# The prompt's W_down as seven block products instead of eight, its combinations made elsewhere

## The chip, the cores and the metric

The kernel runs on one core of a Trainium2 chip. The metric is the time of one execution in device microseconds; a kernel's time is the median of several runs. One further execution was recorded by the hardware profiler. All profile rows of this document come from such recorded executions, and their times count from the start of the recorded span.

The core has five engines with queues of their own: TensorE (PE in the profile, with its weight loads as PEld), VectorE (DVE), ScalarE (ACT), GpSimd (POOL), and SyncE (SP), which here issues most of the DMA transfers and computes nothing. Each engine works through a queue of its own, and what orders one queue against another are semaphores.

## The reference, cut to what matters

One encoder layer runs over two requests, a sample of 512 tokens and a prompt of 1024, with shared weights. The part that this change touches is the MLP at the end of the layer:

```
a = relu(rmsnorm(x, g_mlp) @ w_up)          # (T, 1024) @ (1024, 4096)
y = rmsnorm(x + (a * a) @ w_down, g_final)  # (T, 4096) @ (4096, 1024)
```

Everything is float32. The kernel gets this precision by writing each operand as a sum of two rounded parts, `hi` and `lo`, and by making three matmuls of each product (hi x hi, hi x lo, lo x hi) into one float32 sum.

## The kernel before, in words

The sample runs first, then the prompt. In the order of time the stages that matter are: the sample's MLP (class `Mlp`), in which W_up and W_down alternate in groups of two hidden tiles; the prompt's attention and branches; and the prompt's output projection, W_up and W_down (class `Halves`).

**Splitting.** Both parts of a weight are made on the core. `weights` (L140 ff.) takes one of two buffers named `w_raw` (`wtile`, two buffers for each kind, shared by the whole kernel), loads 512 KB into it by a DMA on SP (L144), and calls `split_sb`: ScalarE writes the rounded copy `hi` (L150), and then GpSimd, or VectorE where `lo_engine` says so, writes `lo` = raw - `hi` (L151). The raw buffer is free when both have read it. `mm3` (L127) issues the three matmuls for each pair of operands.

**The sample's MLP.** `Mlp.run` issues the W_up products of two hidden tiles, and then `down` for the group of two before them. `down` loads the two W_down tiles through `weights`, multiplies, and adds each 128x512 bank of PSUM to an accumulator in SBUF on VectorE (L1080). In every group one tile of the prompt is read, normed and transposed as well.

**The prompt's W_up** (`Halves.up`, from L1346) already works by seven block products instead of eight: halves of the tokens times halves of the inner dimension, in Winograd's form of Strassen's scheme. GpSimd makes the combinations of the weight's quarters beside the products (`prepare`, L1259), ScalarE and GpSimd split them. The result of a group of two hidden tiles is in two tiles `r` and `r_`; after relu and square (L1386) each of them, 128 hidden values by 1024 tokens, is written to DRAM (L1387).

**The prompt's W_down** (`Halves.down`, from L1389) goes over the 32 hidden tiles in 16 groups of two. For each tile it loads the hidden values (128x1024, `lo` on VectorE) and the rows of W_down (128x1024, `lo` on GpSimd). The loads of a group are issued one group ahead, into four pairs of `hi` and `lo` for each kind; the very first go into tiles of the stage before (`take`). A group has 8 token tiles x 2 column halves = 16 banks of six matmuls each, and VectorE adds every bank to an accumulator in SBUF (L1418). The last group adds the final norm (`norm`, L172 to L182) and the output transfers on SP.

**What sets the order.** The program is written in one order, and a planner with estimated durations puts each engine's instructions into its queue: the earliest in the program that it believes to be ready goes next. So an instruction whose operands come late can be passed by a later one, but only at planning time. `pinned` and `behind` tie instructions to a place behind others; `high_priority` moves some ahead. How many buffers a tile's name has is given as `bufs`; a new tile of that name waits until an older one is free.

Of the kernel before, what the change touches and what calls it, by code (L numbers as in the profile page):

```python
# [17 lines left out]
F32 = mybir.dt.float32  # L18
# [8 lines left out]
D = 1024  # L27
# [41 lines left out]
class Layer:  # L69
    def __init__(self, tc, ctx, ins, outs):  # L70
        self.tc, self.nc, self.ins, self.outs = tc, tc.nc, ins, outs
        self.turn = ["mm", "s", "o"]
        self.fn_ready = []
        nc = self.nc
        self.const = ctx.enter_context(tc.tile_pool(name="const", bufs=1))
        self.dram = ctx.enter_context(tc.tile_pool(name="scratch", bufs=1, space=DRAM))
        self.ps = ctx.enter_context(tc.tile_pool(name="ps", bufs=1, space=PSUM))
        self.ident = self.const.tile([128, 128], F32, name="ident")
        make_identity(nc, self.ident)
        self.zero = self.const.tile([128, 8], F32, name="zero")  # L80
# [6 lines left out]
        self.meta_values = None  # L87
        self.lanes = (mybir.EngineType.SP, mybir.EngineType.Activation, mybir.EngineType.Pool, mybir.EngineType.DVE)


# [934 lines left out]
    class Mlp:  # L1025
# [12 lines left out]
        def up(self, f):  # L1038
# [8 lines left out]
            for c in range(T // step):  # L1047
# [7 lines left out]
                nc.vector.tensor_tensor(out=lo[:, cs], in0=r, in1=hi[:, cs].bitcast(F32), op=ALU.subtract)  # L1055
# [45 lines left out]
class Halves:  # L1101

    TH = 512
    NF = FF // 128
    G = 2

    def __init__(self, layer, name, T):
        self.layer, self.nc, self.name, self.T = layer, layer.nc, name, T  # L1110
        self.x = layer.ins[f"x_{name}"]
        self.nt = T // 128
        assert T == 2 * self.TH
        self.sums = [layer.dram.tile([128, D], F32, name=f"sum_{name}{t}") for t in range(self.nt)]
        self.hid = [layer.dram.tile([128, T], F32, name=f"hidden_{name}{f}") for f in range(self.NF)]

    def run(self, right, hp, mp, m, wo):
        layer = self.layer
# [227 lines left out]
    def up(self, mp):  # L1346

        layer, nc, TH = self.layer, self.nc, self.TH
        for g in range(self.NF // 2):
# [32 lines left out]
                pass  # L1382
            nc.scalar.activation(out=r[:, right], in_=r[:, right], func=AF.Relu)
            nc.scalar.activation(out=r_, in_=r_, func=AF.Relu)
            for i, x in enumerate((r, r_)):
                nc.vector.tensor_tensor(out=x, in0=x, in1=x, op=ALU.mult)  # L1386
                nc.sync.dma_start(self.hid[2 * g + i], x)  # L1387

    def down(self, p):  # L1389

        layer, nc, nt, G = self.layer, self.nc, self.nt, self.G
        w, h = {}, {}

        def load(f):
            for x, of, src, lo_engine in (("h", h, self.hid[f], nc.vector), ("w", w, layer.ins["w_down"][f * 128:(f + 1) * 128, :], None)):
                of[f] = layer.weights(src, self.take(2) if f < G else layer.pair(p, [128, D], x, 2 * G), lo_engine=lo_engine)

        for f in range(G):
            load(f)
# [3 lines left out]
        for g in range(self.NF // G):  # L1403
            fs = range(g * G, (g + 1) * G)
            last = fs[-1] == self.NF - 1
            if not last:
                for f in range((g + 1) * G, (g + 2) * G):
                    load(f)
            else:
                gain = layer.gain(p.tile([128, D], F32, name="gain"), "g_final")  # L1410
            for t in range(nt):
                ts = slice(t * 128, (t + 1) * 128)
                for half in range(2):
                    cs = slice(half * 512, (half + 1) * 512)
                    ps = layer.psum()
                    layer.mm3(ps, [(h[f][0][:, ts], h[f][1][:, ts], w[f][0][:, cs], w[f][1][:, cs]) for f in fs])
                    with layer.tc.high_priority(offset=60) if last and t == nt - 1 else nullcontext():
                        nc.vector.tensor_tensor(out=acc[t][:, cs], in0=acc[t][:, cs], in1=ps, op=ALU.add)  # L1418
                if last:
                    o = p.tile([128, D], F32, name="out", bufs=2)  # L1420
                    with layer.tc.high_priority(offset=60) if t == nt - 1 else nullcontext():
                        layer.norm(acc[t], gain, o, junk=p.tile([128, D], BF16, name="junk"))
                    nc.sync.dma_start(layer.outs[self.name][t * 128:(t + 1) * 128, :], o)


def build(tc, ins, outs, order=(("sample", 512), ("prompt", 1024))):
# [84 lines left out]
```

## Time and profile before

| | us |
|---|---|
| median of 3 runs | 2089.66 |
| lowest, highest | 2088.76, 2090.30 |
| profiled execution: its time | 2087.42 |
| profiled execution: its span | 2085.6 |

| engine | busy us | share of the span |
|---|---|---|
| PE | 1999.6 | 96% |
| DVE | 1104.8 | 53% |
| ACT | 704.2 | 34% |
| POOL | 803.6 | 39% |

The recorded span begins and ends a little inside the execution, so the execution's time is 1.8 us above it. Busy shares are averages over stages with different limits. A busy TensorE in this table also says little of how fast its matmuls follow each other: records of matmuls overlap (in the prompt's W_down each is 0.39 us long, and they start 0.23 us apart). The distance between starts is what counts. In rows of a timeline the columns are start and duration in us, the engine, the line of the kernel, the operation with the tile it writes and those it reads, their shapes, and in brackets how long the engine stood idle before it and what ended that. "x4" is a count of like instructions merged into one row, and the duration is then that of all of them. SPq is the queue of SP; the duration there is that of issuing, not that of the transfer.

### The profile page before, as it was taken

The numbers are of one execution on the slowest core, as the hardware profiler recorded it, in microseconds if no ns is written. First come the engines' busy times: TensorE is split into PE (matmuls) and PEld (weight loads), VectorE is DVE, ScalarE is ACT, GpSimd is POOL, SyncE is SP. The second block draws the span as 40 slices with busy tenths as digits, with TensorE's granted clock in tenths as the row PEclk, the third lists the DMA queues.
The fourth block names the chain that finished last, engine by engine and source line by source line (L and its number), as shares of the span: only waits on it lengthen the run. The fifth ranks groups of instructions, "written<-read, shape, count | busy, mean of one in ns | idle before, by whom it ended". The sixth has DMA issues, their size and how long they took to land.

```text
span 2085.6 us, 26699 instructions
## 1 busy us (share of the span) xinstructions
PE 1999.6 (96%) x9803; PEld 1661.5 (80%) x9803; DVE 1104.8 (53%) x2031; ACT 704.2 (34%) x1270; POOL 803.6 (39%) x670
## 2 busy tenths in 40 slices
PE   6789979999999999999999999999999999999997
PEld 4777867878888878888888897877888888888886
DVE  6572435656565454466661328374323336656567
ACT  3464413333332323456642223133333332112112
POOL 2344525243444421333342226027777662222220
PEclk9999999999999999999999999999999999999998
DMA  6555872233433345555463453323323325323322
GB/s 207 163 132 186 224 221 91 82 114 110 123 99 92 94 149 183 130 136 138 122 219 99 128 157 112 118 91 101 107 95 121 107 88 209 108 84 102 100 90 92
DMA packets 244899, 267.25 MB, mean 128 GB/s; under 512 B 41048, under 2 KB 195416, under 8 KB 244216
## 3 DMA queue, kind: packets, MB, share of 16 engines
q1 hardware_dynamic: 231040, 244.67, 37.5%
q0 software_dynamic: 13728, 20.88, 4.2%
q8 instruction: 77, 1.26, 0.3%
q14 instruction: 54, 0.44, 0.1%
HBM read 210.24 MB, written 57.82 MB: 129 GB/s over the span
## 4 chain that ended last, share of the span: by engine, by line
PE 84%; DVE 8%; DMA 3%; ACT 2%; issue 1%; POOL 1%; SPq 1%; DVEq 0%; ACTq 0%; POOLq 0%
PE ps_mm L127 23%; PE ps_o L127 23%; PE ps_s L127 19%; PE ps_t L127 4%; PE ps_mm L491 3%; PE ps_mm L492 3%; PE ps_mm L493 3%; PE ps_o L621 2%; PE ps_t L604 1%; DVE hn L870 1%; DVE gate L875 1%; DMA gain<-in_w_fnB 1%; DMA w_raw<-in_w_out 1%; PE ps_s L591 1%; PE ps_s L592 1%
## 5 line engine op out<-in xcount | busy, mean ns | idle before, releaser
L151 POOL TENSOR_TENSOR w_lo<-w_raw,w_hi 128x1024 fp32r<-128x1024 f32 x141 | 347.0, 2466 | 670.8 <-ACT w_hi L150 620.8
L150 ACT CAST w_hi<-w_raw 128x1024 fp32r<-128x1024 f32 x142 | 147.2, 1047 | 281.2 <-DMA w_raw<-in_w_up 78.2
L1053 DVE TENSOR_TENSOR relu<-relu 128x512 f32<-128x512 f32 (+1 forms) x34 | 78.6, 2312 | 120.5 <-ACT relu L1052 120.5
L491 PE MATMUL ps_mm<-hT,w_hi 128*128 128x512 f32 (+3 forms) x312 | 122.3, 392 | 0.0
L492 PE MATMUL ps_mm<-hT,w_hi 128*128 128x512 f32 (+3 forms) x312 | 112.6, 361 | 0.0
L493 PE MATMUL ps_mm<-hT,w_lo 128*128 128x512 f32 (+3 forms) x312 | 112.5, 361 | 0.0
L150 ACT CAST h_hi<-w_raw 128x1024 fp32r<-128x1024 f32 x30 | 31.5, 1050 | 230.5 <-DMA w_raw<-hidden_prompt 77.3
L598 ACT ACTIVATE sc<-sc,ast 128x288 f32<-128x288 f32 (+4 forms) x96 | 53.8, 561 | 78.5 <-DVE ast L596 78.2
L1418 DVE TENSOR_TENSOR acc<-acc,ps_s 128x512 f32<-128x512 f32 x85 | 58.3, 686 | 39.8 <-PE ps_s L127 39.8
L1418 DVE TENSOR_TENSOR acc<-acc,ps_o 128x512 f32<-128x512 f32 x86 | 59.0, 686 | 38.5 <-PE ps_o L127 38.5
L1418 DVE TENSOR_TENSOR acc<-acc,ps_mm 128x512 f32<-128x512 f32 x85 | 58.3, 686 | 39.3 <-PE ps_mm L127 39.2
L1259 POOL TENSOR_TENSOR x<-w_hi,x 128x512 fp32r<-128x512 f32 (+1 forms) x42 | 63.8, 1519 | 39.5 <-ACT x L1262 39.5
L621 PEld LDWEIGHTS ps_o<-pt,vb 104*64 104x64 f32 (+6 forms) x576 | 63.5, 167 | 11.9 <-ACT pt L131 3.8
L621 PE MATMUL ps_o<-pt,vb 104*64 104x128 f32 (+6 forms) x576 | 66.2, 250 | 5.7 <-ACT pt L131 2.9
L604 PE MATMUL ps_t<-ident,sc 128*104 128x128 f32 (+3 forms) x288 | 50.5, 287 | 17.7 <-DVE pt L132 14.8
L561 POOL TENSOR_TENSOR vb<-vr,vb 96x384 fp32r<-96x384 f32 (+4 forms) x48 | 47.9, 1010 | 48.2 <-ACT vb L560 47.8
L493 PEld LDWEIGHTS ps_mm<-hT,w_lo 128*128 128x128 f32 x312 | 59.6, 191 | 8.3
L127 PE MATMUL ps_t<-gate,x 128*128 128x512 f32 x264 | 65.2, 396 | 0.0
L596 DVE CUSTOM_DVE_ANT_0 sc<-ps_s,bm 128x288 f32<-128x288 f32 (+4 forms) x96 | 46.3, 483 | 33.9 <-PE ps_s L592 18.2
L127 PE MATMUL ps_mm<-gate,x 128*128 128x512 f32 x256 | 64.2, 395 | 0.0
L127 PE MATMUL ps_o<-w_lo,h_hi 128*128 128x512 f32 x160 | 62.2, 389 | 0.0
L127 PE MATMUL ps_s<-w_lo,h_hi 128*128 128x512 f32 x160 | 62.2, 389 | 0.0
(640 smaller groups left out, 5506.4 us busy)
## 6 DMA issues: line engine op xcount, KB each, us to landing
w_raw<-in_w_down SPq DMA_DIRECT2D x64, 512.0 KB
w_raw<-in_w_in SPq DMA_DIRECT2D x56, 512.0 KB
w_raw<-in_w_up SPq DMA_DIRECT2D x34, 512.0 KB
w_raw<-hidden_prompt SPq DMA_DIRECT2D x32, 512.0 KB
w_raw<-in_w_out SPq DMA_DIRECT2D x16, 512.0 KB
hidden_prompt<-r_hi SPq DMA_DIRECT2D x16, 512.0 KB
hidden_prompt<-r_lo SPq DMA_DIRECT2D x16, 512.0 KB
w_lo<-in_w_up SPq DMA_DIRECT2D x15, 512.0 KB
```

What stands on the lines that cost most here:

```text
L127: self.nc.tensor.matmul(out, a, b, start=(i == 0 and not more), stop=(i == len(terms) - 1), skip_group_check=more)
L150: nc.scalar.copy(out=hi, in_=raw)
L151: (lo_engine or nc.gpsimd).tensor_tensor(out=lo, in0=raw, in1=hi.bitcast(F32), op=ALU.subtract)
L491: nc.tensor.matmul(ps, a[0], b[0], start=(kt == 0), stop=False)
L492: nc.tensor.matmul(ps, a[0], b[1], start=False, stop=False)
L493: nc.tensor.matmul(ps, a[1], b[0], start=False, stop=(kt == 7))
L598: nc.scalar.activation(out=sc[:, :W], in_=sc[:, :W], func=AF.Exp, bias=st[:, 0:1], scale=-1.0, accum_out=st[:, 1:2])
L604: nc.tensor.transpose(tp[:ck, c * 128:(c + 1) * 128], sc[:, c * ck:(c + 1) * ck], self.ident)
L621: nc.tensor.matmul(po[:m, j * 128:(j + 1) * 128], v, x, start=(i == 0), stop=(i == len(ops) - 1))
L1053: nc.vector.tensor_tensor(out=r, in0=r, in1=r, op=ALU.mult)
L1259: self.nc.gpsimd.tensor_tensor(out=to, in0=x, in1=y, op=op)
L1418: nc.vector.tensor_tensor(out=acc[t][:, cs], in0=acc[t][:, cs], in1=ps, op=ALU.add)
```

## The change

The prompt's W_down becomes seven block products, too. The operand blocks are halves of the tokens by halves of the inner dimension (the two 128-row tiles of a group form the two halves), times halves of the inner dimension by halves of the columns. Eight combinations are needed of the hidden values' four blocks and of the weight's four blocks, four each.

- *Hidden values.* After the squares, `Halves.up` makes four combinations s1 to s4 of 128x512 per group on VectorE, in two tiles `h0` and `h1`, and writes four instead of two 512 KB pieces to DRAM, ordered by block.
- *Weights.* `Mlp.down`, which loads all of W_down for the sample anyway, makes the combinations t1 to t4 of each pair of raw tiles on GpSimd (`combine`, in the two `hn` tiles) and writes them to DRAM in two pieces per pair. To that end the raw tile of the even one is kept until the odd one's combinations are made.
- *The products.* `Halves.down` runs seven products, one after the other, over eight units of the inner dimension (512 rows each): 56 steps. A step loads one hidden block (`[128, 2, 512]`, 512 KB) and one weight block (the same), two steps ahead, through `weights` as before, and multiplies for four token tiles of 128: per token tile one bank and six matmuls. A product stays in its four banks over all eight steps. Three products go on in the banks of an earlier one (`more`). Only behind the eighth step are the four banks read: by ScalarE once, otherwise by VectorE, with running sums `u2` and `u3`. One half of the tokens is finished after the sixth product, the other after the seventh, whose last three steps are multiplied together, one token tile after the other.

The diff, cut to its core; the three functions named `down`, `up` and `down` in it are `Mlp.down`, `Halves.up` and `Halves.down`:

```diff
+        def combine(self, g, even, odd):
+            nc, wt = self.nc, self.layer.wt
+            if g % 2 == 0:
+                wt.append(self.layer.dram.tile([128, 2, 4, 512], F32, name=f"wt{g // 2}"))
+            (b11, b12), (b21, b22) = ([x[:, i] for i in range(2)] for x in (even, odd))
+            t = [self.hp.tile([128, D], F32, name="hn", bufs=2) for _ in range(2)]
+            t1, t2, t3, t4 = (x[:, i * 512:(i + 1) * 512] for x in t for i in range(2))
+            for to, x, y in ((t1, b12, b11), (t2, b22, t1), (t3, b22, b12), (t4, b21, t2)):
+                nc.gpsimd.tensor_tensor(out=to, in0=x, in1=y, op=ALU.subtract)
+            for i, x in enumerate(t):
+                nc.sync.dma_start(wt[-1][:, g % 2, 2 * i:2 * i + 2].rearrange("p a b -> p (a b)"), x)
...
     def down(self, fs, last, gate):
-                w[f] = [t.rearrange("p a b -> p (a b)") if T == 512 else t for t in layer.weights(
-                    layer.ins["w_down"][f * 128:(f + 1) * 128, :].rearrange("p (a b) -> p a b", a=2), to)]
+                raw = layer.wtile("raw", [128, 2, 512]).bitcast(F32)
+                nc.sync.dma_start(raw, layer.ins["w_down"][f * 128:(f + 1) * 128, :].rearrange("p (a b) -> p a b", a=2))
+                w[f] = [t.rearrange("p a b -> p (a b)") if T == 512 else t for t in layer.split_sb(raw, *to)]
+                if f % 2:
+                    self.combine(f // 2, even, raw)
+                even = raw
...
     def up(self, mp):
             for i, x in enumerate((r, r_)):
                 nc.vector.tensor_tensor(out=x, in0=x, in1=x, op=ALU.mult)
-                nc.sync.dma_start(self.hid[2 * g + i], x)
+                nc.sync.dma_start(to[:, i * 2 * TH:(i + 1) * 2 * TH], x)
+            h = [self.tile(f"h{i}") for i in range(2)]
+            s1, s2, s3, s4 = (x[:, y] for x in h for y in (left, right))
+            for k, x, y, op in ((s1, r[:, right], r_[:, right], ALU.add), (s2, s1, r[:, left], ALU.subtract),
+                                (s3, r[:, left], r[:, right], ALU.subtract), (s4, r_[:, left], s2, ALU.subtract)):
+                nc.vector.tensor_tensor(out=k, in0=x, in1=y, op=op)
+            for i, x in enumerate(h, 2):
+                nc.sync.dma_start(to[:, i * 2 * TH:(i + 1) * 2 * TH], x)
...
+    DOWN = ((0, "b11", 0), (5, "t2", 1), (2, "b21", 0), (6, "t3", 1), (4, "t1", 0), (3, "t4", 1), (7, "b22", 0))
     def down(self, p):
+        steps = [(n, u) for n in range(len(self.DOWN)) for u in range(nu)]
+        def load(i):
+            n, u = steps[i]
+            a, b, _ = self.DOWN[n]
+            got[n, u] = [layer.weights(src, [three(x) for x in self.take(2)] if i < 2 else layer.pair(p, [128, 2, 512], k, 4),
+                                       lo_engine=lo) for k, src, lo in (("h", self.hid[u][:, :, a], nc.vector), ("w", block(b, u), None))]
+        def evict(n, t):
+            ps = banks[self.DOWN[n][2]][t]
+            c1, c2 = acc[t], acc[nh + t]
+            if n == 0:
+                nc.scalar.copy(out=u2[t], in_=ps)
+            elif n == 1:
+                add(u2[t], u2[t], ps)
+            elif n == 2:
+                add(c1[:, left], c1[:, left], ps)
+                add(c1[:, right], c1[:, right], u2[t])
...
+            elif n == 5:
+                add(c2[:, left], c2[:, left], ps)
+                finish(nh + t)
...
+        apart = 3
+        for i, (n, u) in enumerate(steps):
+            at = self.DOWN[n][2]
+            if u == 0 and n in (0, 1, 3, 4):
+                banks[at] = [layer.psum(k) for k in (("mm", "s"), ("t", "o"))[at] for _ in range(2)]
+            load(i + 2)
+            if n == len(self.DOWN) - 1 and u >= nu - apart:
+                continue
+            for t in range(nh):
+                product(banks[at][t], t, n, [u])
+            if u == nu - 1:
+                for t in range(nh):
+                    evict(n, t)
+        for t in range(nh):
+            product(banks[0][t], t, len(self.DOWN) - 1, list(range(nu - apart, nu)))
+            evict(len(self.DOWN) - 1, t)
```

More of the change, by code (lines that the diff above doesn't have):

```diff
@@ L87, in __init__ @@
         self.meta_values = None
+        self.wt = []
         self.lanes = (mybir.EngineType.SP, mybir.EngineType.Activation, mybir.EngineType.Pool, mybir.EngineType.DVE)
@@ L1114, in __init__ @@
         self.sums = [layer.dram.tile([128, D], F32, name=f"sum_{name}{t}") for t in range(self.nt)]
-        self.hid = [layer.dram.tile([128, T], F32, name=f"hidden_{name}{f}") for f in range(self.NF)]
+        self.hid = [layer.dram.tile([128, 2, 8, self.TH], F32, name=f"hidden_{name}{u}") for u in range(self.NF // 4)]
     def run(self, right, hp, mp, m, wo):
@@ L1384, in up @@
             nc.scalar.activation(out=r_, in_=r_, func=AF.Relu)
+            to = self.hid[g // 2][:, g % 2].rearrange("p q t -> p (q t)")
             for i, x in enumerate((r, r_)):
                 nc.vector.tensor_tensor(out=x, in0=x, in1=x, op=ALU.mult)
-                nc.sync.dma_start(self.hid[2 * g + i], x)
-    def down(self, p):
[L1391 to L1399, printed above, removed]
+                nc.sync.dma_start(to[:, i * 2 * TH:(i + 1) * 2 * TH], x)
@@ L1402, in down @@
             nc.sync.dma_start(acc[t], self.sums[t])
[L1403 to L1408, printed above, removed]
-            else:
[L1410 to L1423, printed above, removed]
@@ new lines, in down, with finish @@
+        gain = layer.gain(p.tile([128, D], F32, name="gain"), "g_final")
+        u2, u3 = ([p.tile([128, TH], F32, name=f"u{k}{t}") for t in range(nh)] for k in (2, 3))
+        left, right = slice(0, TH), slice(TH, 2 * TH)
+        add = lambda to, x, y: nc.vector.tensor_tensor(out=to, in0=x, in1=y, op=ALU.add)
+        banks = [None, None]
+        def finish(t, urgent=False):
+            o = p.tile([128, D], F32, name="out", bufs=2)
+            with layer.tc.high_priority(offset=60) if urgent else nullcontext():
+                layer.norm(acc[t], gain, o, junk=p.tile([128, D], BF16, name="junk"))
+            nc.sync.dma_start(layer.outs[self.name][t * 128:(t + 1) * 128, :], o)
```

28 lines of the change are left out of this document (added).

## The prediction

> **What bounds the kernel now.** I began with busy time by stretches of the span, because this change touches three stages (the sample's MLP, the prompt's W_up, the prompt's W_down) whose limits need not be the same. Then came the chain of waits through the last stage, and last the instructions of ScalarE, GpSimd and the load queue there. Of a row of stretches the columns are the stretch, its length, and the busy time of PE, weight load, DVE, ACT and POOL with counts, then the granted clock, the DMA share and GB/s; the rows of the chain are start, length, engine.
>
> ```profile
> span 2085.6 us, 26699 instructions
> 1800.00:1900.00 100.00, 100.00 (x443) 82.84 (x442) 59.41 (x82) 18.40 (x18) 22.68 (x10) 1.00 0.28 91
> 1750.24 1.36 PE ps_mm L127 x6
> 1751.60 1.36 PE ps_s L127 x6
> ```
>
> In the prompt's W_down TensorE never stops, at full clock, and every bank of six matmuls follows the last by 1.36 us: 0.227 us per matmul. A group of two hidden tiles is 16 banks, 21.8 us, and 16 groups make the stage. ACT and POOL work a fifth of the time. So the stage is TensorE's, and fewer matmuls are worth time, but only as long as the operands arrive. How fast can they? The next rows are one group: start, length, engine, instruction, and in brackets the idle time before it with its releaser.
>
> ```profile
> 1854.09 1.05 ACT L150 CAST h_hi<-w_raw 128x1024 fp32r<-128x1024 f32 x1 [11.99 <-PE ps_s L127]
> 1855.05 1.04 ACT L150 CAST w_hi<-w_raw 128x1024 fp32r<-128x1024 f32 x1
> 1860.34 1.05 ACT L150 CAST h_hi<-w_raw 128x1024 fp32r<-128x1024 f32 x1 [4.25 <-DMA w_raw<-hidden_prompt]
> 1862.81 1.05 ACT L150 CAST w_hi<-w_raw 128x1024 fp32r<-128x1024 f32 x1 [1.42 <-DMA w_raw<-in_w_down]
> 1856.16 2.92 POOL L151 TENSOR_TENSOR w_lo<-w_raw,w_hi 128x1024 fp32r<-128x1024 f32 x1 [11.58 <-ACT w_hi L150]
> 1863.93 2.40 POOL L151 TENSOR_TENSOR w_lo<-w_raw,w_hi 128x1024 fp32r<-128x1024 f32 x1 [4.85 <-ACT w_hi L150]
> 1856.85 0.33 SPq L144 DMA_DIRECT2D w_raw<-hidden_prompt  x1
> 1859.11 0.33 SPq L144 DMA_DIRECT2D w_raw<-in_w_down  x1
> 1862.67 0.33 SPq L144 DMA_DIRECT2D w_raw<-hidden_prompt  x1
> 1866.36 0.33 SPq L144 DMA_DIRECT2D w_raw<-in_w_down  x1
> ```
>
> This is the row set on which the forecast rests. All loads go through `w_raw`, which has two buffers, and SP takes hidden, weight, hidden, weight in turn. A weight load issued at 1859.11 is cast from 1862.81 (3.70 us), its low part is made on POOL from 1863.93 to 1866.33, and the next weight load goes out at 1866.36, 0.03 us after the buffer is free. Nothing else was waited for. The loop through one buffer is therefore **7.25 us**: 3.70 landing, 1.05 cast, 0.07, 2.40 low part, 0.03. The hidden loop, whose low part is DVE's, goes from 1856.85 to 1862.67, 5.82 us. Now each loop turns twice in 21.8 us and then ACT waits 11.99 us for TensorE. This slack is not visible in any share of busy time.
>
> **The change part by part.**
>
> *Matmuls.* Before: 16 groups x 16 banks x 6 = 1536. After: 7 products x 8 units x 4 token tiles x 6 = 1344. The 192 removed are worth 192 x 0.227 = 43.5 us while TensorE sets the pace.
>
> *Loads of W_down: the term that decides.* Before, 32 hidden and 32 weight loads of 512 KB. After, each of 56 steps needs one of each: 56 and 56, because a product uses only half the tokens with half the columns. One step is 4 banks, 4 x 1.36 = 5.44 us of TensorE. Yet `wtile` is untouched, there are still two raw buffers, and both splits stay with their engines. Loading two steps ahead into four pairs does not help: a queue in front of a loop of 7.25 us gives one weight per 7.25 us. So from the first steps on a step should cost 7.25 and not 5.44 us.
>
> Does the new form of the transfer alter 3.70? The rows are now 2 KB and not 4 KB. The trace has such loads, those of W_out:
>
> ```profile
> 1263.68 3.20 SPq L144 DMA_DIRECT2D w_raw<-in_w_out  x2
> 1267.26 1.05 ACT L150 CAST w_hi<-w_raw 128x1024 fp32r<-128x1024 f32 x1 [2.96 <-DMA w_raw<-in_w_out]
> ```
>
> 3.58 us, so no. I keep 3.70. Beside these rows stands a rule of the Trainium skill, "DMA: Bandwidth & Descriptors", section "Anatomy of one DMA": about 2.0 us that do not depend on size, plus bytes over 436 GB/s, which for 512 KB is an estimate of 3.2 us. By it the loop would be 6.75 us and the sum below 51 x 0.5 = 25 us less; the rows decide.
>
> Bounds of the loop: if the two buffers swapped roles at each step, two loads would share both loops, (5.82 + 7.25) / 2 = 6.54. Upward, POOL's 2.92 in place of 2.40 gives 7.77. The longer span comes where DVE's `h_lo` holds POOL up; the order the other way is this:
>
> ```profile
> 1744.74 2.41 POOL L151 TENSOR_TENSOR w_lo<-w_raw,w_hi 128x1024 fp32r<-128x1024 f32 x1 [10.90 <-ACT w_hi L150]
> 1745.42 2.81 DVE L151 TENSOR_TENSOR h_lo<-w_raw,h_hi 128x1024 fp32r<-128x1024 f32 x1
> 1754.09 2.41 POOL L151 TENSOR_TENSOR w_lo<-w_raw,w_hi 128x1024 fp32r<-128x1024 f32 x1 [6.94 <-ACT w_hi L150]
> ```
>
> DVE started inside POOL's instruction, and ended 1.08 us after it. I take 7.25: on SP the next hidden load can only go out behind the weight load, so it lands later, its low part falls behind POOL's, and the weight loop keeps its 2.40.
>
> *The sum.* The start should be as now: the two first loads (steps 0 and 1) go ahead through tiles of `take`, and then pairs fill behind the eight `acc` loads. Of the weights in pairs the one split at 1744.74 is the second and the one at 1754.09 the third; by steps that is step 4, ready at 1754.09 + 2.41 = 1756.50. From there 51 steps to the last, 51 x 7.25 = 369.8: **2126.3**. The three last steps are multiplied together by token tile, so 63 of their 72 matmuls still follow the last weight: 63 x 0.227 = 14.3, **2140.6**. Then the tail:
>
> ```profile
> 2071.94 0.61 PE L127 MATMUL ps_o<-w_hi,h_lo 128*128 128x512 f32 x2
> 2072.82 0.68 DVE L1418 TENSOR_TENSOR acc<-acc,ps_o 128x512 f32<-128x512 f32 x1
> 2074.11 1.06 ACT L172 ACTIVATE junk<-acc 128x1024 bf16<-128x1024 f32 x1
> 2080.66 1.28 DVE L182 SCALAR_TENSOR_TENSOR out<-acc,st,gain 128x1024 f32<-128x1024 f32 x1 [0.42 <-DMA out_prompt<-out]
> ```
>
> Now it is 2085.6 - 2072.55 = 13.05 us, with two other norms queued ahead. After, a token tile comes every 18 x 0.227 = 4.1 us, so less queues; the bounds are 8 and 13, I take 10.5: **2151**.
>
> *Evictions.* 256 adds of PSUM at 686 ns, 176 us of DVE, become 36 adds and 4 copies.
>
> ```profile
> L1418 DVE TENSOR_TENSOR acc<-acc,ps_o 128x512 f32<-128x512 f32 x86 | 59.0, 686 | 38.5 <-PE ps_o L127 38.5
> ```
>
> They are no gain, since they lie beside TensorE now. The new ones run while the next product uses the other four banks; cover gone, each wait is 4 x 0.69. After the sixth product, four norms with outputs stand on DVE, ACT and SP ahead of later low parts and loads: between 0 and 12 us, and I take 4.
>
> *Combinations beside W_up.* Per group four DVE adds of 128x512 and two more writes of 512 KB. The stage, and the nearest DVE row with both inputs in SBUF:
>
> ```profile
> 1440.00:1700.00 260.00, 260.00 (x1117) 209.51 (x1116) 87.07 (x93) 88.53 (x137) 192.38 (x137) 1.00 0.33 107
> L1055 DVE TENSOR_TENSOR hid_lo<-relu,hid_hi 128x512 fp32r<-128x512 f32 (+1 forms) x32 | 20.9, 654 | 11.0 <-ACT hid_hi L1054 10.6
> L1259 POOL TENSOR_TENSOR w_hi<-w_hi 128x512 f32<-128x512 f32 x14 | 18.1, 1292 | 1.1
> ```
>
> 16 x 4 x 0.65 = 42 us for a DVE that is a third busy; TensorE covers it. Against POOL, 74% busy, each can wait 1.29 us. The adds end a group; what they delay is the first PSUM add of the next, and that bank has a second buffer. 1 us, between 0 and 5; a hidden tile written late is not read before the W_down stage.
>
> *Combinations in the sample's MLP.* 64 POOL subtractions (the 1.29 us above) and 32 writes; both raw buffers of a pair now stay taken until t3 and t4 are made.
>
> ```profile
> 521.15 4.79 POOL L151 TENSOR_TENSOR w_lo<-w_raw,w_hi 128x1024 fp32r<-128x1024 f32 x2 [8.19 <-ACT w_hi L150]
> 528.70 2.40 POOL L151 TENSOR_TENSOR w_lo<-w_raw,w_hi 128x1024 fp32r<-128x1024 f32 x1 [2.76 <-ACT w_hi L150]
> 533.34 2.40 POOL L151 TENSOR_TENSOR w_lo<-w_raw,w_hi 128x1024 fp32r<-128x1024 f32 x1 [2.23 <-ACT w_hi L150]
> 523.59 2.76 SPq L144 DMA_DIRECT2D w_raw<-in_w_up  x2
> 520.17 5.50 PE ps_o L127 x24
> 532.10 1.40 PE ps_s L127 x6
> 543.03 5.50 PE ps_mm L127 x24
> ```
>
> The W_down pair is split by 525.94 and used at 532.10: 6.2 us spare. The buffers then take W_up, ready at 531.10, used at 543.03: 11.9 us spare, in a period of 22.86. The combinations cost 4 x 1.29 = 5.2 us per pair; ahead of the splits or behind them they fit either margin. Cover gone, it is 16 x 5.2 = 83. The last pairs have no W_up behind them, so up to 5 us there. I take 3, between 0 and 10. What also queues behind a combination is SP's write of it and every load after that write. A rule speaks against this part: the Trainium skill, "SBUF — State Buffer", section "Who interferes with whom", has DVE and GpSimd take one port pair in turns, the loser blocked for a whole instruction. The rows of `h_lo` agree (2.81 for 1.23). By it each subtraction could also stop a DVE instruction of this stage for 1.29 us, 64 x 1.29 = 83 us of DVE; without a bank that waits for DVE the sum stays.
>
> Together 2151 + 4 + 1 + 3 = 2159 us of span. The profiled run took 2087.42 us, 1.8 above its span, and the median of the runs, 2089.66, is 2.2 above that: **2163 us**, 3.5% slower.
>
> **The rivals.**
>
> *Buffers swap roles, 6.54 us a step:* 51 x 0.71 = 36 less, 2127. For it: nothing but the order of freeing ties a buffer to a kind of load. Against it: the four SP rows alternate strictly.
>
> *The sample is load-bound too:* if the combinations stand ahead of the splits, the chain of the buffers closes on itself: from W_up's issue at 523.59 to its second split done at 535.74 are 12.15, landing of W_down 3.70, combinations 5.17, split 2.40, together 23.4 against 22.86. That eats the 6.2 us in some eleven pairs; with the bounds of the sample's end and a few gaps about 15 us more, 2178. Against it: POOL idles 8.19 us before each pair of splits, just where the combinations can go.
>
> *The other side, loads stay hidden.* The place is again the raw loop: if it turns in 5.44 us or less, TensorE sets the pace, 2085.6 - 43.5 - 2.5 (tail) + 8 = 2048 span, 2052 us. It decides from 5.8 us a step: (2159 - 2085.6) / 51 = 1.44 under 7.25 is no change. For it: 1 MB per 5.44 us is only 193 GB/s, while the hidden loop alone is at 5.82. Against: the weight loop holds 3.45 us on ACT and POOL alone, so the landing would have to take 2 us, and no row shows it. The Trainium skill, "DMA: Bandwidth & Descriptors", section "Specifications", has 435 GB/s for the engines together; by bandwidth alone it is this rival.
>
> **How the numbers follow.** Forecast 0.66, sample too 0.09, swapped buffers 0.12, other side 0.13 (faster 0.10, same 0.03, with 0.2% as about what a measurement of this kernel can tell). So slower 0.87. The forecast's own range is 2147 to 2190: down with all small terms at their low ends (10 us) and W_out's landing of 3.58 (51 x 0.12 = 6), up with POOL's 2.92 in two steps of three (17) and half of the small terms' upper ends (10). The whole range takes in the swapped buffers and the sample, and leaves out the other side: 2110 to 2195.
>
> **What would show it.** After: in W_down, weight loads on SP about 7.25 us apart with POOL `w_lo` as releaser, ACT `w_hi` waiting for its DMA in nearly every step, TensorE busy some 75% (5.44 of 7.25), its idle time put down to `w_lo`; the last matmul some 75 us later than now. W_up and the sample's MLP should keep their TensorE at 99 to 100%. Weight loads 5.5 us apart with a full TensorE would make the forecast wrong at its root; gaps in the sample before W_down products would add to it.

## The result and the profile after

The change makes the kernel slower, as forecast, but by twice as much: **2238.01 us** against 2089.98 us of the kernel before on the same chip, ratio 1.0706 [1.0688, 1.0725]. The forecast was 2163 us. The profiled execution has a span of 2238.7 us, 153.1 above that of before.

Where do the 153 us lie? Three instructions on SP serve as marks: the last outputs of the sample, and the first and the last write of a group's `r_hi` in W_up. Columns of the timeline rows are start, duration, queue, instruction. Before:

```profile
755.62 10.94 SPq L1085 DMA_DIRECT2D out_sample<-hn  x3
1434.67 0.34 SPq L1387 DMA_DIRECT2D hidden_prompt<-r_hi  x1
1723.00 0.32 SPq L1387 DMA_DIRECT2D hidden_prompt<-r_hi  x1
```

After:

```profile
span 2238.7 us, 26384 instructions
807.49 10.96 SPq L1103 DMA_DIRECT2D out_sample<-hn  x3
1489.14 0.49 SPq L1409 DMA_DIRECT2D hidden_prompt<-r_hi  x1
1780.74 0.32 SPq L1409 DMA_DIRECT2D hidden_prompt<-r_hi  x1
```

| stretch | before | after | longer | forecast |
|---|---|---|---|---|
| up to the sample's end | 766.6 | 818.5 | 51.9 | 3 |
| from there to the first `r_hi` | 668.1 | 670.7 | 2.6 | 0 |
| W_up, first to last `r_hi` | 288.3 | 291.6 | 3.3 | 1 |
| from the last `r_hi` to the end (W_down) | 362.6 | 458.0 | 95.4 | 69 |

So there are two causes, not one. The view of busy time by stretches shows both. Its rows are the sample's MLP, W_up and W_down; the columns are as in the prediction (PE, weight load, DVE, ACT, POOL, clock, DMA share, GB/s):

```profile
440.00:720.00 280.00, 258.43 (x1141) 205.78 (x1140) 140.70 (x230) 85.02 (x122) 164.20 (x88) 1.00 0.41 134
1510.00:1770.00 260.00, 259.90 (x1116) 208.65 (x1115) 190.23 (x149) 86.13 (x134) 211.95 (x131) 1.00 0.46 163
1810.00:2210.00 400.00, 320.49 (x1219) 235.99 (x1220) 110.54 (x123) 113.02 (x114) 123.44 (x52) 0.95 0.45 141
```

TensorE is idle a fifth of W_down; a quarter was forecast. But it is also idle for 21.6 of 280 us in the sample's MLP, which was to stay full.

**W_down.** The chain of waits through two neighbouring steps, one with weights from the input and one with weights from the scratch array `wt`:

```profile
1956.89 3.52 DMA w_raw<-in_w_down
1960.52 1.06 ACT w_hi L151
1961.64 2.39 POOL w_lo L152
1964.05 4.61 DMA w_raw<-wt
1968.76 1.05 ACT w_hi L151
1969.88 2.38 POOL w_lo L152
1972.27 4.09 DMA w_raw<-wt
```

This is the loop of the forecast, link by link: load, cast, low part, and 0.02 us later the next load of a weight. With `in_w_down` it takes 1964.05 - 1956.89 = 7.16 us, with `wt` 8.22. How many steps are of which sort is told by the low parts of the weights, one for each step (the view of one tile: count, shortest, median and longest in ns, first and last start in us):

```profile
L152 POOL TENSOR_TENSOR w_lo<-w_raw,w_hi x52: 2348/2372/3231, 1818.0 to 2216.4; 128x1024 fp32r<-128x1024 f32 x52
...
L152 POOL TENSOR_TENSOR w_lo<-w_raw,w_hi x9: 2362/2372/2382, 1903.7 to 1961.6; 128x1024 fp32r<-128x1024 f32 x9
L152 POOL TENSOR_TENSOR w_lo<-w_raw,w_hi x25: 2360/2372/2860, 1961.6 to 2154.7; 128x1024 fp32r<-128x1024 f32 x25
```

The first row spans the 51 steps from step 4 to the last, 398.4 us instead of 369.8. The second row spans the eight steps of a product with weights from the input: 57.9 / 8 = **7.24 us** (forecast 7.25). The third spans 24 steps with weights from `wt`: 193.1 / 24 = **8.05 us**.

**The sample's MLP.** One period of the group, on ScalarE (one row), POOL and then SP:

```profile
579.01 1.04 ACT L151 CAST w_hi<-w_raw 128x1024 fp32r<-128x1024 f32 x1
...
581.38 1.29 POOL L1068 TENSOR_TENSOR hn<-w_raw 128x512 f32<-128x512 f32 x1 [3.49 <-issue]
582.63 2.82 POOL L152 TENSOR_TENSOR w_lo<-w_raw,w_hi 128x1024 fp32r<-128x1024 f32 x1
589.03 1.31 POOL L1068 TENSOR_TENSOR hn<-w_raw,hn 128x512 f32<-128x512 f32 x1 [3.58 <-DMA w_raw<-in_w_down]
...
592.85 4.79 POOL L152 TENSOR_TENSOR w_lo<-w_raw,w_hi 128x1024 fp32r<-128x1024 f32 x2
...
569.80 2.79 SPq L145 DMA_DIRECT2D w_raw<-in_w_up  x2
577.92 7.90 SPq L1081 DMA_DIRECT2D w_raw<-in_w_down  x2
595.27 2.78 SPq L145 DMA_DIRECT2D w_raw<-in_w_up  x2
```

The loads of W_up now go out every 595.27 - 569.80 = 25.47 us; before it was 22.86. Read the rows as a circle. The second W_up tile has its rounded copy at 580.05 (ACT), but in POOL's queue its low part stands behind subtraction t1, and t1 waits for the even W_down tile, issued at 577.92 and there at 581.38 (the view names no releaser here; in the periods at 451.39 and 477.38 us it names that load). So the low part starts at 582.63, some 2.5 us after its operands were ready. That tile's raw buffer is free at 585.45, and only then can the odd W_down tile be loaded (the second of the two issues at 577.92 ends at 585.82). It is there at 589.03. Three subtractions need it, the two splits stand behind these, until 597.64; the first one's end lets the next W_up load go at 595.27. The circle's links are 15.65 us from W_up's issue to the second split's end, 3.58 of landing, 3.82 for the three subtractions and 2.42 for the split with the release: 25.47, one behind the other.

### The profile page after: what moved, and what is told of

It reads as the page before. It is cut to its first block, busy times and chain, and to the rows that moved or that the text cites. A ratio compares the mean times of both kernels' runs of the same rounds, so it can differ in the third digit from the quotient of the medians.

```text
span 2238.7 us, 26384 instructions
## 1 busy us (share of the span) xinstructions
PE 2023.9 (90%) x9611; PEld 1641.4 (73%) x9611; DVE 1106.9 (49%) x1899; ACT 756.8 (34%) x1322; POOL 970.5 (43%) x758
## 2 busy tenths in 40 slices
DMA packets 275362, 325.96 MB, mean 146 GB/s; under 512 B 42840, under 2 KB 197208, under 8 KB 274680
## 4 chain that ended last, share of the span: by engine, by line
PE 39%; DMA 11%; POOL 8%; DVE 4%; ACT 4%; issue 2%; SPq 0%; POOLq 0%; ACTq 0%; DVEq 0%
PE ps_mm L128 9%; PE ps_o L128 9%; POOL w_lo L152 7%; PE ps_s L128 6%; DMA w_raw<-wt 5%; DMA w_raw<-in_w_down 5%; PE ps_t L128 4%; ACT w_hi L151 3%; PE ps_mm L492 2%; PE ps_mm L493 2%; PE ps_mm L494 2%; PE ps_o L622 1%; PE ps_t L605 1%; POOL hn L1068 1%; DVE hn L871 1%
## 5 line engine op out<-in xcount | busy, mean ns | idle before, releaser
L152 POOL TENSOR_TENSOR w_lo<-w_raw,w_hi 128x1024 fp32r<-128x1024 f32 x165 | 404.6, 2457 | 610.0 <-ACT w_hi L151 571.7
L151 ACT CAST w_hi<-w_raw 128x1024 fp32r<-128x1024 f32 x166 | 173.7, 1048 | 539.7 <-DMA w_raw<-in_w_up 133.1
L152 DVE TENSOR_TENSOR h_lo<-w_raw,h_hi 128x1024 fp32r<-128x1024 f32 x54 | 79.5, 1473 | 263.8 <-ACT h_hi L151 263.8
L1054 DVE TENSOR_TENSOR relu<-relu 128x512 f32<-128x512 f32 (+1 forms) x34 | 53.3, 1567 | 170.0 <-ACT relu L1053 170.0
L151 ACT CAST h_hi<-w_raw 128x1024 fp32r<-128x1024 f32 x54 | 56.6, 1048 | 100.3 <-DMA w_raw<-hidden_prompt 95.5
L1280 POOL TENSOR_TENSOR x<-w_hi,x 128x512 fp32r<-128x512 f32 (+1 forms) x42 | 78.7, 1874 | 22.8 <-ACT x L1283 22.8
L128 PE MATMUL ps_mm<-w_lo,h_hi 128*128 128x512 f32 x120 | 54.5, 457 | 35.3 <-POOL w_lo L152 35.3
L128 PE MATMUL ps_t<-w_lo,h_hi 128*128 128x512 f32 x96 | 45.3, 471 | 28.2 <-POOL w_lo L152 28.1
L128 PE MATMUL ps_mm<-w_hi,h_hi 128*128 128x512 f32 x120 | 48.3, 437 | 19.1 <-ACT w_hi L151 19.0
L1068 POOL TENSOR_TENSOR hn<-w_raw,hn 128x512 f32<-128x512 f32 x32 | 42.7, 1334 | 50.9 <-DMA w_raw<-in_w_down 50.9
```

Of the source, the lines that this page charges most:

```text
L128: self.nc.tensor.matmul(out, a, b, start=(i == 0 and not more), stop=(i == len(terms) - 1), skip_group_check=more)
L151: nc.scalar.copy(out=hi, in_=raw)
L152: (lo_engine or nc.gpsimd).tensor_tensor(out=lo, in0=raw, in1=hi.bitcast(F32), op=ALU.subtract)
L1054: nc.vector.tensor_tensor(out=r, in0=r, in1=r, op=ALU.mult)
L1068: nc.gpsimd.tensor_tensor(out=to, in0=x, in1=y, op=ALU.subtract)
L1280: self.nc.gpsimd.tensor_tensor(out=to, in0=x, in1=y, op=op)
```

## The experiments

**Four raw buffers in W_down.** The changed kernel, but raw loads of W_down alternate between the tiles named `w_raw` and those named `w_hi`, which stand empty in that stage.

```diff
-    def weights(self, src, to=None, scale=1.0, lo_engine=None):
+    def weights(self, src, to=None, scale=1.0, lo_engine=None, kind="raw"):
...
-        raw = self.wtile("raw", shape).bitcast(F32)
+        raw = self.wtile(kind, shape).bitcast(F32)
...
-                                       lo_engine=lo) for k, src, lo in
+                                       lo_engine=lo, kind=('raw', 'hi')[i % 2]) for k, src, lo in
```

> The changed kernel with one difference: in the prompt's W_down stage the raw loads alternate between the two `w_raw` buffers and the two `w_hi` ones that stand idle there, so four raw buffers instead of two. Theory (the loop through two raw buffers sets the step): with four a step falls from about 7.2 to 8.2 us to TensorE's 5.5, the stretch from the last write of `r_hi` to the end goes from 458 to about 330, the kernel from 2238 to about 2112. Rival (the transfers themselves are the limit, 1 MB per step with landings of 4.5 us and more): steps stay above 6.5 us, the stretch above 390, the kernel above 2170.

Measured: 2112.49 us, ratio to the kernel before 1.0103 [1.0074, 1.0133]. The stretch of W_down falls from 458.0 to 331.8 us (from 1779.1 to the end at 2110.9). Busy time, and the load queue in the middle of a product with `wt`:

```profile
1790.00:2090.00 300.00, 293.58 (x1272) 241.75 (x1272) 116.09 (x129) 114.71 (x120) 134.76 (x54) 0.98 0.65 209
...
1902.95 0.52 SPq L145 DMA_DIRECT2D w_raw<-wt  x1
1908.30 0.52 SPq L145 DMA_DIRECT2D w_hi<-wt  x1
1913.73 0.52 SPq L145 DMA_DIRECT2D w_raw<-wt  x1
```

A weight load goes out every 5.4 us, TensorE's pace, at 209 GB/s. Nothing about the work or the transfers was altered, only the number of buffers: the loop is the cause, and 126 us hang on it. The rival, engines or transfers that cannot follow, is out. The stretch is now 30.8 us shorter than before the change, so the fewer matmuls are worth something; and the kernel is still slower than before, as the sample still ends 51.0 us late (817.6 against 766.6).

**Scratch arrays laid out by block.** The changed kernel, two raw buffers, but a block of `wt` or of the hidden values is one contiguous piece of DRAM; in the change its 2 KB pieces lie between those of the other blocks (8 KB from piece to piece in `wt`, 16 KB in the hidden values).

```diff
-                wt.append(self.layer.dram.tile([128, 2, 4, 512], F32, name=f"wt{g // 2}"))
+                wt.append(self.layer.dram.tile([4, 128, 2, 512], F32, name=f"wt{g // 2}"))
...
-        self.hid = [layer.dram.tile([128, 2, 8, self.TH], F32, name=f"hidden_{name}{u}") for u in range(self.NF // 4)]
+        self.hid = [layer.dram.tile([8, 128, 2, self.TH], F32, name=f"hidden_{name}{u}") for u in range(self.NF // 4)]
```

> The changed kernel with one difference: the two scratch arrays in DRAM are laid out block by block, so that a load of a `wt` or hidden block reads 512 KB in one piece instead of 2 KB rows that lie 8 or 16 KB apart (and the writes are in 2 KB rows instead). Theory (the scattered rows make `wt` land in 4.0 to 4.75 us instead of 3.5): landings of `wt` return to about 3.6, the 32 steps that use it lose 0.9 us each, the kernel falls by 25 to 32 us to about 2209. Rival (they are slow because the array was written by the kernel, or because two transfers are under way at once): no change, 2238 within 5.

Measured: 2217.81 us, ratio 1.0607 [1.0576, 1.0638]. The same 24 steps with `wt`, and their loads on the chain:

```profile
L152 POOL TENSOR_TENSOR w_lo<-w_raw,w_hi x25: 2362/2374/2385, 1958.1 to 2132.9; 128x1024 fp32r<-128x1024 f32 x25
...
1968.37 3.44 DMA w_raw<-wt
1982.49 3.49 DMA w_raw<-wt
```

174.8 / 24 = 7.28 us: the loop of the forecast, now for `wt` too. The stretch of W_down becomes 432.3 us, 25.7 shorter; the forecast was 432. So the layout is what the forecast of this stage lacked. Two things about it changed at once: the pieces of a block lie together, and they are larger. The packets of a whole execution go from 275362 to 276386; the difference of 1024 is what comes out when each of the 96 writes of these arrays takes 128 packets more and each of the 88 loads 128 fewer, that is, when a load reads 128 pieces of 4 KB instead of 256 of 2 KB. The whole gained 20.2 us, less than the stretch, as the stages ahead of it became 3.4 us longer in the profiled execution (1784.1 against 1780.7 to the last `r_hi`); why stays open.

**The rows padded by 64 bytes.** Is it the distance, a power of two, or that the pieces lie apart at all? Here they stay apart, but each has 528 elements instead of 512, in `wt` as in the hidden values (shown for `wt`).

```diff
-                wt.append(self.layer.dram.tile([128, 2, 4, 512], F32, name=f"wt{g // 2}"))
+                wt.append(self.layer.dram.tile([128, 2, 4, 528], F32, name=f"wt{g // 2}")[:, :, :, :512])
```

> The changed kernel with one difference: the scratch arrays keep their order, but each 2 KB row is followed by 64 unused bytes, so the rows of a block lie 8.25 or 16.5 KB apart instead of 8 or 16. It parts two readings of the gain by the block-wise layout (2238 to 2218). Theory (strides of a power of two send the rows to few places of the DRAM): landings of `wt` fall to 3.6 us as they did block-wise, about 2218. Rival (rows that lie apart are slow as such): landings stay at 4.0 to 4.75, the kernel within 5 us of 2238.

Measured: 2231.04 us, ratio 1.0681 [1.066, 1.0702]. The 24 steps:

```profile
L152 POOL TENSOR_TENSOR w_lo<-w_raw,w_hi x25: 2358/2380/2396, 1962.8 to 2146.8; 128x1024 fp32r<-128x1024 f32 x25
```

184.0 / 24 = 7.67 us, half way between 8.05 and 7.28, and the stretch of W_down is 444.1 us, 13.9 shorter. (The whole gains only 7.0, as the sample ended some 5 us later.) About half of the loss goes with the padding, at the same size of the pieces; neither reading alone holds. Whether the other half comes from the distance that is left or from the size of the pieces stays open. Size alone is not it: W_down's own blocks, read in 2 KB pieces 4 KB apart from partition to partition, take 7.24.

**The sample's part alone.** The kernel before, with `combine` and its writes added to `Mlp.down` as in the change; nothing reads `wt`, and W_up and W_down of the prompt are those of before.

```diff
+                raw = layer.wtile("raw", [128, 2, 512]).bitcast(F32)
+                nc.sync.dma_start(raw, layer.ins["w_down"][f * 128:(f + 1) * 128, :].rearrange("p (a b) -> p a b", a=2))
...
+                if f % 2:
+                    self.combine(f // 2, even, raw)
+                even = raw
```

> The kernel before plus the combinations in the sample's MLP alone, with their writes, which nothing reads. Theory (the combinations close a chain through the two raw buffers in the sample): the group period there goes from 22.9 to about 25.4 us, the sample's end moves by 50 to 54 us, the kernel comes to about 2142. Rival (the sample loses time only together with the other parts): under 2100.

Measured: 2144.32 us, ratio 1.0256 [1.0226, 1.0286]. The stretch up to the sample's end is 51.9 us longer, to a tenth as in the change. The loss of the sample's MLP is made by this part alone.

**The sample's raw tiles elsewhere.** The changed kernel, but the W_down pair goes into the two `hn` tiles and not into `w_raw`, and the subtractions are made there in place. POOL has the same 64 subtractions, SP the same writes; the shared raw buffers are left to W_up. The order on POOL changes as well: in place, the subtractions can only follow the splits of their own tiles, so t1 no longer stands ahead of W_up's split.

```diff
-                raw = layer.wtile("raw", [128, 2, 512]).bitcast(F32)
+                raw = self.hp.tile([128, D], F32, name="hn", bufs=2).rearrange("p (a b) -> p a b", a=2)
...
-            for to, x, y in ((t1, b12, b11), (t2, b22, t1), (t3, b22, b12), (t4, b21, t2)):
+            for to, x, y in ((b11, b12, b11), (b12, b22, b12), (b22, b22, b11), (b21, b21, b22)):
```

> The changed kernel with one difference: in the sample's MLP the raw W_down tiles get the two `hn` buffers, the combinations are made in place there, and W_up keeps the two `w_raw` buffers for itself; the GpSimd work and the writes stay. Theory (shared raw buffers): the period returns to about 22.9 us, the kernel falls by 40 to 52 us to about 2190. Rival (GpSimd's 5.2 us per pair, with its blocking of VectorE, or the writes are what costs): the period stays above 25, the kernel within 10 us of 2238.

Measured: 2204.49 us, ratio 1.0544 [1.0508, 1.0579]. Busy time, the load queue and POOL:

```profile
440.00:720.00 280.00, 280.00 (x1262) 230.33 (x1261) 177.49 (x246) 97.14 (x134) 197.04 (x102) 1.00 0.44 151
...
584.97 0.38 SPq L145 DMA_DIRECT2D w_raw<-in_w_up  x1
585.41 1.05 SPq L1080 DMA_DIRECT2D hn<-in_w_down  x2
607.83 0.38 SPq L145 DMA_DIRECT2D w_raw<-in_w_up  x1
...
594.66 4.77 POOL L152 TENSOR_TENSOR w_lo<-hn,w_hi 128x1024 fp32r<-128x1024 f32 x2 [6.89 <-ACT w_hi L151]
599.39 6.05 POOL L1066 TENSOR_TENSOR hn<-hn 128x512 f32<-128x512 f32 x4
```

The period is 607.83 - 584.97 = 22.86 us again, both W_down loads go out in one stroke, and TensorE is full, with POOL busier than in the change. The subtractions as such cost nothing in this steady part. The loss came from their hold on W_up's buffers, with t1 ahead of W_up's split; the edit takes away both at once, and no run parts them. The sample's end is at 779.6, 13.1 later than before, instead of 51.9. The expectation was a gain of 40 to 52 us, and the whole gained 34: the sample gave back 38.8, but W_down, where only the order of the four pieces in `wt` is another, took 464.2 us, 6.2 longer. Why stays open.

**All three together.** Six raw buffers in W_down (`w_raw`, `w_hi`, `w_lo` in turn), the layout by block, and the `hn` tiles: the three edits above, with `kind=('raw', 'hi', 'lo')[i % 3]`.

> The changed kernel with three differences together: six raw buffers in the prompt's W_down stage (`w_raw`, `w_hi` and `w_lo` in turn), the scratch arrays block by block, and the sample's W_down raw tiles in `hn` with the combinations in place. Theory (the two raw loops are the whole loss): 2112 less the 34 that the sample gave back, less up to 2 for the landings, now hidden: about 2077, 0.993 of the kernel before. Rival (what one part gives back the others take again, through transfers at a higher rate): 2090 or more.

Measured: 2078.53 us, ratio 0.9951 [0.9934, 0.9968]: half a per cent under the kernel before. A second form put the last two W_down tiles of the sample into `w_raw`, to clear the end of that stage:

```diff
-                raw = self.hp.tile([128, D], F32, name="hn", bufs=2).rearrange("p (a b) -> p a b", a=2)
+                raw = (self.hp.tile([128, D], F32, name="hn", bufs=2).rearrange("p (a b) -> p a b", a=2) if i < 2 else
+                       layer.wtile("raw", [128, 2, 512]).bitcast(F32))
```

> As the one before, but the last two W_down tiles of the sample, which no W_up load follows, take the free `w_raw` buffers instead of waiting for `hn`. Theory (the 13 us that the sample still loses lie mostly at its end, in the waits for `hn`): about 2069, 0.990 of the kernel before. Rival (the weight loads of the prompt, which then wait for these buffers, start the prompt late by as much): no better than the one before.

Measured: 2078.58 us, 0.9944 [0.9924, 0.9963], no gain, as its rival had it. Where does the first one still wait? Its chain at the start of W_down:

```profile
1752.53 5.84 DMA acc<-sum_prompt
1758.44 10.34 DMA w_lo<-in_w_down
1769.97 2.37 POOL w_lo L152
```

The weights of the third step are queued behind the eight loads of `acc`, 4 MB, of which nothing is needed before the third product.

**Loads of `acc` later.** The second form, with `acc` loaded one tile per step from step 10 on, and the subtractions of the sample's last group behind its splits in the program.

```diff
+            for pair in pairs:
+                self.combine(*pair)
...
-        for t in range(nt):
-            nc.sync.dma_start(acc[t], self.sums[t])
...
             load(i + 2)
+            if 8 <= i < 16:
+                with layer.pinned():
+                    nc.sync.dma_start(acc[i - 8], self.sums[i - 8])
```

> As the kernel with six raw buffers, scratch by blocks and the last two W_down tiles of the sample in w_raw (2078.6 us), but (a) the four subtractions of either pair of the sample's last group follow all four splits of that group, and (b) the eight loads of acc at the start of the prompt's W_down stand behind the loads of steps 10 to 17, one each, since the third product is the first to read them. Theory: the sample's remaining 13 us over the kernel before are for the most part combinations ahead of splits at its end (about 9), and the start of W_down waits some 6 to 12 us for loads queued behind acc; the time becomes about 2062 us, ratio 0.987, the sample's end 771 us or earlier, and the W_down stage 325 to 330 us. Rival: POOL has to do the 16 subtractions before it is free for the next stage's low parts and the stage of W_down starts no earlier, as its first loads wait for buffers and not for the queue; then 2075 to 2080, ratio 0.994.

Measured: 2064.76 us, ratio 0.9881 [0.9865, 0.9898]. The same place in the chain:

```profile
1748.96 6.72 DMA w_lo<-in_w_down
1756.88 2.39 POOL w_lo L152
```

The third step is ready 13 us earlier than in the first form (10 against the last `r_hi`), and the stretch of W_down is 323.7 us instead of 335.9 there and 337.3 in the second form. The other half of the edit brought little: the sample's end is at 779.8 after 780.9 in the second form, where 771 was expected. POOL shows that the planner had put the first pair's subtractions ahead of the last splits all the same:

```profile
732.61 6.09 POOL L1066 TENSOR_TENSOR hn<-hn 128x512 f32<-128x512 f32 x4
738.66 2.35 POOL L152 TENSOR_TENSOR gate<-w_raw,gate 128x1024 fp32r<-128x1024 f32 x1
```

**The last subtractions tied behind the splits.**

```diff
             for pair in pairs:
-                self.combine(*pair)
+                with layer.pinned() if last else nullcontext():
+                    self.combine(*pair)
```

> As the kernel of 2064.8 us, whose four last combinations the planner still put ahead of the two last splits of the sample (POOL: combinations 732.6 to 738.7, split, two more, split until 746.7, with 5.9 us of TensorE waits for them): now the eight subtractions of the last group are tied behind all four splits. Theory: the last split ends 6.1 + 3.3 = 9.4 us earlier, and TensorE gets back its wait of 5.9 us and what stands empty beside it between 740 and 760 (5.0 of 20), so 5 to 6 us: about 2059.5 us, ratio 0.985. Rival: the subtractions now stand ahead of the next stage's splits on POOL (at 753 and 760, with 4.9 to 6.2 us of idle time before each) and of the free hn tiles of the outputs, and the time stays at 2063 to 2066.

Measured: **2063.51 us**, ratio 0.9873 [0.9856, 0.9889]. POOL, what TensorE waits for between 715 and 785 us (sum, times, longest), and SP:

```profile
734.46 5.24 POOL L152 TENSOR_TENSOR gate<-w_raw,gate 128x1024 fp32r<-128x1024 f32 x2 [1.85 <-ACT gate L151]
739.66 6.15 POOL L1066 TENSOR_TENSOR hn<-hn 128x512 f32<-128x512 f32 x4
745.76 5.40 POOL L1066 TENSOR_TENSOR w_raw<-w_raw 128x512 f32<-128x512 f32 x4
...
PE ps_mm L128 <- POOL r L152: 1.9, 1, 1.9
PE ps_mm L128 <- ACT r L151: 1.9, 1, 1.9
...
751.65 3.09 SPq L145 DMA_DIRECT2D w_raw<-in_w_in  x2
```

The subtractions now follow all splits, and the wait for `gate` (5.9 us in the run before) is gone. But the time is only 1.3 us lower where 5 to 6 were expected, and the intervals of the two ratios overlap, so a gain is not shown. The first loads of the next stage now stand on SP behind the write of the last combinations (made by 751.2) and go out at 751.65, in the run before at 749.87; TensorE waits 3.8 us for `r`, the low and high parts of the next stage's weights. The wait moved on by one stage, and the time lies within what the rival said, 2063 to 2066.

## Why the prediction was wrong in size

The sign was right, and so was the mechanism forecast for W_down. Two terms of the sum failed; of the 79.7 us between the forecast span (2159) and the measured one they make 48.9 and 25.6.

**"I take 3, between 0 and 10" for the sample: 51.9 were measured.** The failed step is the sentence "ahead of the splits or behind them they fit either margin". The margins of 6.2 and 11.9 us were taken between a split and the product that uses it, and compared with 5.2 us of POOL work. But the change did more to this stage than add work: the odd tile's and the even tile's raw buffers now stay taken until all subtractions are made, and they are the buffers through which W_up is loaded too. What had to be compared was the circle through the buffers with the period of 22.86 us. The prediction did work it out, as the rival "the sample is load-bound too", and got 23.4 us. It took W_up's second split to be done 12.15 us after W_up's issue, as before; measured are 15.65, because the planner put t1 ahead of that split. t1 reads only the even tile, but it had to wait for that tile's landing, and with it waited the release of the very buffer that the odd tile needed. In return only three subtractions are left behind the landing, not four. An estimate from these links: with t1 behind that split the circle would be 25.47 - 2.5, about 23.0 us, hardly longer than the period. By this estimate it takes the shared buffers and this order together; no run has the one without the other, so that is not shown. From the W_up loads at 413.91 us (418.91 after the change) to the last ones at 703.74 (746.87) the lag grows from 5.0 to 43.1 us; the other 8.8 come behind them. Against this rival stood "POOL idles 8.19 us before each pair of splits": idle time of an engine is no evidence when the order on it is a planner's and the operands come later. The runs show the part (its edit alone loses the same 51.9 us), and that with other buffers and the order that goes with them the steady loss is gone.

The rule of the Trainium skill weighed there, "SBUF — State Buffer", section "Who interferes with whom", would have DVE and GpSimd block each other. It explains little of the loss here: the split behind t1 takes 2.82 us instead of 2.40, at most 0.42 of the 2.61 us that this period is longer, and with the raw tiles in `hn`, POOL at 197.04 and DVE at 177.49 of 280 us, TensorE stays at 280.00.

**"3.58 us, so no. I keep 3.70" for the landing: 3.86 to 4.75 us for `wt`, 4.35 in the mean.** A load of W_out has pieces of 2 KB like one of `wt`, and I took the size of a piece for all that mattered. Where the pieces lie was not compared: 4 KB apart in W_out, 8 KB apart in `wt`. 32 steps at 8.05 - 7.25 = 0.80 us are 25.6. Blocks that are contiguous bring 7.28, so it is shown that the layout makes it. What about the layout does so is narrowed down for half of it only, by the padding. By the rule of the Trainium skill quoted there, "DMA: Bandwidth & Descriptors", section "Anatomy of one DMA", every one of these loads would take an estimated 3.2 us; the traces have 3.4 to 3.5 at best. The fit of that section is for DMAs issued from GpSimd, and these loads are issued on SP.

**What held.** The term that decides, two raw buffers and a loop of 7.25 us: 7.24 measured for weights from the input, with the releaser named, and 5.4 with four buffers. The rival that buffers swap roles (6.54) does not occur. The other side, loads hidden behind two buffers, does not occur either. The norms in the middle: the last eight steps span 2216.4 - 2154.7 = 61.7 us,

```profile
L152 POOL TENSOR_TENSOR w_lo<-w_raw,w_hi x9: 2361/2370/3231, 2154.7 to 2216.4; 128x1024 fp32r<-128x1024 f32 x9
```

which is 3.7 above 8 x 7.25; 4 were taken. Start and end of the stage missed by a few us in opposite ways and nearly cancel, which is luck: step 4 was ready 39.7 us after the last `r_hi`, not 33.5, and from the last low part to the end it took 19.9 us, not 14.3 + 10.5. W_up lost 3.3 instead of 1, within its bounds.

**Where the gain of 43.5 us is.** It exists, and the final form has it for the most part: its marks are 775.0, 1445.0, 1736.4 and 2061.0.

```profile
span 2061.0 us, 26420 instructions
771.57 3.46 SPq L1107 DMA_DIRECT2D out_sample<-hn  x2
1445.02 0.53 SPq L1413 DMA_DIRECT2D hidden_prompt<-r_hi  x1
1736.42 0.37 SPq L1413 DMA_DIRECT2D hidden_prompt<-r_hi  x1
```

W_down takes 324.6 us, 38.0 less than before; 10.3 are lost up to the first `r_hi`, 8.5 of them by the sample's end, and 3.1 in W_up. Together 24.6 less, the difference of the spans.

## What to carry to other kernels

When a change makes a buffer be held longer, or makes more loads pass through it, work out the whole circle through that buffer (load, cast, low part, release, next load), in the order in which the engines' queues will really have it, and compare it with the period; the spare time between a result and its user does not tell it. Fewer matmuls with more loads need more raw buffers first: from two to four was worth 126 us here, at no other change. Where a scratch array is one's own, lay it out as it will be read, and on a queue look at what goes ahead of the first operands of a stage.

## What was not expected of the hardware

Loads of 512 KB take unlike times by how the block lies in DRAM. With `wt` (2 KB pieces, 8 KB from start to start) a step of the loop is 8.05 us, with 64 bytes of padding behind each piece 7.67, with contiguous blocks (4 KB pieces) 7.28, and with half rows of W_down from the input (2 KB pieces, 4 KB apart from partition to partition) 7.24. With one load after another in the loop this goes straight into the time; with four buffers the loads from the same arrays cost nothing, 5.4 us a step.
